# Loading the out-projection's weights into u's places during the last projection group, and 24 out-projection steps ahead of attention

## The chip, the cores and the metric

The kernel runs on one core of one Trainium2 chip. The metric is the device time of one execution in microseconds (us); lower is better. The core has five engines with a queue of their own each: TensorE (PE, with its weight loads shown as PEld), VectorE (DVE), ScalarE (ACT), GpSimd (POOL) and SyncE (SP), which here issues nearly all DMAs. An engine works through its queue in the order that was fixed when the kernel was built.

## The reference

One layer of a decoder with three parallel branches. `x` is 2048 tokens by 1024, `w_in` has 5656 columns, `w_out` is 2048 by 1024, all float32:

```
u    = rms_norm(x, norm_g)
q, k, v, z_att, f, z_ssd, xbc, dt, x_lru, z_lru = split(u @ w_in)
y_att = fox_attention(q, k, v, f) * silu(z_att)      # 8 heads of 64, causal, forget-gate bias
y_ssd = ssd(conv(xbc), dt, z_ssd), rms-normed        # 16 heads of 64, state 128
y_lru = rglru(conv(x_lru)) * silu(z_lru)             # 512 channels, a scan over time
out  = x + concat(y_att 512, y_ssd 1024, y_lru 512) @ w_out
```

## The kernel before

**Precision.** A matmul on fp32 data is made of three passes on rounded parts: a matrix is split into a high part `h` (a cast on ACT) and a low part `l` = raw - h (a subtraction on DVE or POOL), and the product is hh + hl + lh. So each weight and each input costs a cast and a subtraction before PE can use it.

**Stages.** (1) `x` is normalised, transposed and split into `uh` and `ul`: four blocks `tb` of 512 tokens, eight tiles of 128 x 512 each, 128 KB per partition in all, in the pool `up`. (2) Groups of 256 columns of `w_in` are loaded (`weights`) and multiplied with all of u, with convolutions, scans and gates behind them; results go to DRAM. (3) The SSD units. (4) For each of four pairs of heads a q/k group (tiles `pqk`, `ptq`, `sth`, `stl`) and a v/z group (`group_vz`: eight steps `t2` of 256 tokens, accumulator `pvz`, results `vs` and `zt`, stored as `v_d` and `za_d`). Steps 1 and 2 of a v/z group read u's block 0, steps 3 and 4 block 1, and so on. Three accumulator buffers (`psj`) serve these groups; `vs` has five buffers, `zt` two. (5) `pb.close()` gives back u, the weights' pools and the accumulators, and attention's pools are laid out in their place: `a4` (the logits `L`), `o2` (`mh`, `ml`, `xr`), `a2`, `a3` (`ph`, `pl`), `wo` (the split half of `w_out`, 64 KB per partition), `o1` (the raw inputs `mt`), `kvB`. (6) Attention together with the first out-projection sweep. (7) The second sweep.

**Attention.** 64 units, one for each head and block `sb` of 256 queries; heads' blocks go down (7 to 0) for the first and the last head and up for the others. `logits` makes the steps of a unit: a chunk of 512 keys at a time, PE makes `S` (L814, L815), DVE subtracts the bias and keeps the maximum (L816), ACT takes the exponential of the whole row (L820). `attend` goes over pairs of key tiles (`kp`): PE transposes `L` into `T` (L869), ACT and DVE split it into `ph` (L876) and `pl` (L877), PE multiplies with v into `O` (L855, L856), and the chunks of the next unit are put between. At the unit's end come `os`, the transposes `pf` and the sum `ats`, stored as `at_d`. The chunks of the very first unit are made with raised priority, and the keys, values and biases of the next head (`kh`, `vv`, `cb`) are loaded in each head's third unit.

**Out-projection.** `sweep` is a generator; one `next` is one step. A step multiplies one 128-row block `k` of `w_out` with a token tile's input for 256 output columns: three matmuls (L977, L979, L981) into the accumulator `po`, of which the first sweep has one (`psP`). Eight steps make one 256-wide output, which DVE adds into `xr` by two instructions (L985, L988); 32 steps make a token tile of 128. `mix` loads a tile's input (`mt`, one buffer for each half: one load from `gt_d`, four from `lr_d`), casts it to `mh` on ACT (L956) and subtracts to `ml` on POOL (L957); it is called one tile ahead. The first sweep (rows 1024 to 2047 of `w_out`: 512 steps) fills attention: after each of the 288 kp steps `fill` issues as many steps as keep it in proportion:

```
count[0] += 1
want = count[0] * 512 // 288
while want > count[1]: ... next(filler, None)
```

The generator starts, and with it `mix` of the first two tiles, at the first `fill`. The second sweep (rows 0 to 1023) has its own 512 steps after attention.

**`load_wo`** loads a half of `w_out` and splits it: eight row blocks `k`; a raw row block of 512 KB lies in the place of the next block's `wol`, the last one in the two `mt` buffers; each is split in two pieces of 512 columns (ACT L921 or L925, DVE L922 or L926). Before, it is called after the first unit's chunks and again after attention.

**Order.** All instructions are put in an order per engine by a planner that simulates the kernel with costs of its own, taking among what is ready the one that comes first in the program (raised priority counts as earlier). A tile that takes over another's place waits for that tile's last user alone (`reuse_waits`).

Of the kernel before, what the change touches and what calls it, by code (L numbers as in the profile page):

```python
# [8 lines left out]
F32 = mybir.dt.float32  # L9
F32R = mybir.dt.float32r  # L10
I32 = mybir.dt.int32
BF16 = mybir.dt.bfloat16
AF = mybir.ActivationFunctionType
ALU = mybir.AluOpType
# [4 lines left out]
P = 128  # L19
S = 2048  # L20
D = 1024
NT = S // P
# [5 lines left out]
NSL = 9  # L28
NQ = 4
QB = 5  # L30
ZPOOL = True
LORD = "x0 x1 z0 g0 x2 z1 g1 x3 z2 z3 g2 g3"
LAG = 4
# [11 lines left out]
def hybrid_block(ctx, tc, x, norm_g, w_in, q_norm_g, k_norm_g, forget_b, ssd_conv_w, ssd_conv_b,  # L45
# [3 lines left out]
    def tpool(**kw):  # L49
        if kw.get("space") is not DRAM:  # L50
            kw["reuse_waits"] = "tile"
        return tc.tile_pool(**kw)
# [100 lines left out]


    pb = ExitStack()
    up = pb.enter_context(tpool(name="up", bufs=1))
    psY = pb.enter_context(tpool(name="psY", bufs=3, space=PSUM))
    pst = pb.enter_context(tpool(name="pst", bufs=2, space=PSUM))
    psj = pb.enter_context(tpool(name="psj", bufs=3, space=PSUM))
# [2 lines left out]

    uh, ul = [], []
    for tb in range(4):
        uh.append([up.tile([P, 512], F32R, name=f"uh{tb}_{k}", tag=f"uh{tb}_{k}")
                   for k in range(KD)])
        ul.append([up.tile([P, 512], F32R, name=f"ul{tb}_{k}", tag=f"ul{tb}_{k}")
                   for k in range(KD)])
# [25 lines left out]
    with tpool(name="p0", bufs=2) as p0, tpool(name="p01", bufs=1) as p01, \  # L194
# [44 lines left out]
        def c1(name, i=0):  # L239
            j = CV[name] + i  # L240
            return cv[:, j:j + 1]
# [475 lines left out]
    def load_q(h, sb):  # L717
# [8 lines left out]
            dma(ql[u * 64:u * 64 + 64, :].bitcast(F32), qk_d["q", "l", p][hs, qs])  # L726
        heads[h][3:] = [qh, ql]

    with tpool(name="ap", bufs=2) as pool, tpool(name="ap1", bufs=1) as ap1, \
            tpool(name="qkp", bufs=QB) as qkp:  # L730
        for p in range(4):
            w = weights([(C_Q + p * P, P), (C_K + p * P, P)])
            for th in range(8 // NQ):
                ss = pool.tile([P, NQ, 8], F32, name=f"sqk{p}_{th}", tag="sqk")
                rs = pool.tile([P, NQ, 8], F32, name=f"rqk{p}_{th}", tag="rqk")
                qks = []
                for i in range(NQ):
                    t2 = th * NQ + i
                    qk = qkp.tile([P, 2, 256], F32, name=f"qk{p}_{t2}", tag="qk")
                    qks.append(qk)  # L740
                    ps = proj_tok2(w, t2, f"pqk{p}_{t2}")
                    A.copy(qk, ps)
                    sq = ap1.tile([P, 2, 256], F32, name=f"sq{p}_{t2}", tag="sqq")
                    A.activation(sq, ps, AF.Square)
                    V.tensor_reduce(ss[:, i, :], sq.rearrange("p i (h d) -> p (i h) d", d=64),
                                    axis=AX.X, op=ALU.add)
                s2_, r2_ = (z.rearrange("p a b -> p (a b)") for z in (ss, rs))
                V.tensor_scalar(s2_, s2_, 1.0 / 64.0, EPS, op0=ALU.mult, op1=ALU.add)
                rsqrt(ap1, r2_, s2_, NQ * 8, f"rk{p}{th}")
                for i, qk in enumerate(qks):  # L750
                    t2 = th * NQ + i
                    qv = qk.rearrange("p i (h d) -> p (i h) d", d=64)
                    V.tensor_tensor(qv, qv, rs[:, i, :].unsqueeze(2).broadcast_to([P, 8, 64]),
                                    op=ALU.mult)
                    pt = pst.tile([P, 2, 256], F32, name=f"ptq{p}_{t2}", tag="pt")
                    for j in range(2):
                        for i2 in range(2):
                            T.transpose(pt[:, j, i2 * P:(i2 + 1) * P],
                                        qk[:, i2, j * P:(j + 1) * P], ident)
                    ts = slice(t2 * 256, (t2 + 1) * 256)  # L760
                    for j, (wn, gn) in enumerate((("q", "qg"), ("k", "kg"))):
                        sh = pool.tile([P, 256], F32R, name=f"sth{p}_{t2}_{j}", tag="sth")
                        sl = pool.tile([P, 256], F32R, name=f"stl{p}_{t2}_{j}", tag="stl")
                        A.activation(sh, pt[:, j, :], AF.Copy, scale=c1(gn))
                        V.scalar_tensor_tensor(sl, pt[:, j, :], c1(gn), sh.bitcast(F32),
                                               op0=ALU.mult, op1=ALU.subtract)
                        dma(qk_d[wn, "h", p][:, ts], sh.bitcast(F32))
                        dma(qk_d[wn, "l", p][:, ts], sl.bitcast(F32))
            if p > 0:
                group_vz(pool, qkp, p)  # L770
            if p == 2:
                load_head(0)
                load_q(*units[0])
    pb.close()

    pcx = ExitStack()
# [1 line left out]
    o2 = cx.enter_context(tpool(name="o2", bufs=2))  # L778
    a2 = cx.enter_context(tpool(name="a2", bufs=2))
    a3 = cx.enter_context(tpool(name="a3", bufs=3))  # L780
    wo = cx.enter_context(tpool(name="wo", bufs=1))
    o1 = cx.enter_context(tpool(name="o1", bufs=1))
    kvB = cx.enter_context(tpool(name="kvB", bufs=1))
    psS = pcx.enter_context(tpool(name="psS", bufs=PB[0], space=PSUM))
# [115 lines left out]

    pt_d = dram("pt_d", [S, D])

    def load_wo(ks):
        w = {}
        for j, k in enumerate(ks):
            h = wo.tile([P, D], F32R, name=f"woh{k}", tag=f"woh{j}")
            l = wo.tile([P, D], F32R, name=f"wol{k}", tag=f"wol{j}")
            row = w_out[k * P:(k + 1) * P, :]
            if j < 7:
                whole = wo.tile([P, D], F32, name=f"wor{k}", tag=f"wol{j + 1}")  # L910
                dma(whole, row)
            for n in range(2):
                cs = slice(n * 512, n * 512 + 512)
                if j < 7:
                    raw = whole[:, cs]
                else:
                    raw = o1.tile([P, 512], F32, name=f"wor{k}_{n}", tag=f"mt{n}")
                    dma(raw, row[:, cs])
                if 4 <= k < 12:
                    g = c1("sg", k - 4)  # L920
                    A.activation(h[:, cs], raw, AF.Copy, scale=g)  # L921
                    V.scalar_tensor_tensor(l[:, cs], raw, g, h[:, cs].bitcast(F32),  # L922
                                           op0=ALU.mult, op1=ALU.subtract)
                else:
                    A.copy(h[:, cs], raw)  # L925
                    V.tensor_tensor(l[:, cs], raw, h[:, cs].bitcast(F32),  # L926
                                    op=ALU.subtract)
            w[k] = (h, l)
        return w

    def sweep(w, psP, psX, parts, resid, dst, ts):


# [27 lines left out]
        for i, t in enumerate(ts):  # L961
            nxt = mix(ts[i + 1]) if i + 1 < NT else None
            tsl = slice(t * P, (t + 1) * P)
            mh, ml = cur
            for n in range(4):
                cs = slice(n * 256, n * 256 + 256)
                if n % 2 == 0:
                    xr = o2.tile([P, 512], F32, name=f"xr{t}_{n}_{ks[0]}", tag="xr")
                    dma(xr, resid[tsl, n * 256:n * 256 + 512])
                xc = xr[:, n % 2 * 256:n % 2 * 256 + 256]  # L970

                ps = psP.tile([P, 2, 256], F32, name=f"po{t}_{n}_{ks[0]}", tag="P")
                for j, k in enumerate(ks):
                    yield
                    h, l = w[k]
                    o = ps[:, j // 4, :]
                    T.matmul(o, mh[:, j, :], h[:, cs], start=(j == 0), stop=False,  # L977
                             skip_group_check=True)
                    T.matmul(o, mh[:, j, :], l[:, cs], start=False, stop=False,  # L979
                             skip_group_check=True)  # L980
                    T.matmul(o, ml[:, j, :], h[:, cs], start=False, stop=(j % 4 == 3),  # L981
                             skip_group_check=True)
                for j, (kind, _) in enumerate(parts):
                    if kind in (0, 1):
                        V.scalar_tensor_tensor(xc, ps[:, j, :], rsn[:, t, kind:kind + 1], xc,  # L985
                                               op0=ALU.mult, op1=ALU.add)
                    else:
                        V.tensor_tensor(xc, xc, ps[:, j, :], op=ALU.add)  # L988
                if n % 2:
                    dma(dst[tsl, n * 256 - 256:n * 256 + 256], xr)  # L990
            cur = nxt

    with tc.high_priority(offset=HP):
        cur, steps = logits(*units[0])
        for st in steps:
            st()
    w = load_wo(range(8, 16))
    filler = sweep(w, psP, None, ((1, 8), ("lru", 12)), xf, pt_d, range(NT))
    count = [0, 0]
    recent = []  # L1000

    def fill(ins):
# [14 lines left out]
    pcx.close()  # L1017
    psP2 = cx.enter_context(tpool(name="psP2", bufs=5, space=PSUM))
    psX = cx.enter_context(tpool(name="psX", bufs=3, space=PSUM))
    w = load_wo(list(range(4, 8)) + list(range(0, 4)))  # L1020
    for _ in sweep(w, psP2, psX, ((0, 4), ("att", 0)), pt_d, of, range(NT - 1, -1, -1)):
        pass
    cx.close()

# [28 lines left out]
```

## Time and profile before

| | us |
|---|---|
| median of 3 runs (2082.02, 2083.0, 2092.18) | 2083.0 |
| the profiled execution | 2094.4 |
| its span, first to last instruction | 2092.4 |
| PE busy in it | 2011.2 |
| DVE busy | 1278.1 |
| ACT busy | 954.3 |
| POOL busy | 542.0 |
| first start and last end of a split instruction of w_out, first half | 1276.7 and 1297.6 |
| last v/z result taken by ACT | 1275.49 |
| first out-projection matmul | 1306.7 |
| first out-projection matmul of the second sweep | 1898.12 |

All numbers come from one profiled execution, which is 0.5% above the median of the runs. Times inside are counted from the first instruction. Busy time of an engine counts its instructions alone; a busy PE isn't PE at its peak, since matmuls overlap and run at half speed where the granted clock is 0.50. Rows of DMAs on SP (SPq) show the issue, not the transfer.

### The profile page before, as it was taken

Reading aid. Unit: us, or ns where it says so; the run is one execution under the profiler, and the core shown is the slowest. Engines: PE = TensorE matmul, PEld = TensorE weight load, DVE = VectorE, ACT = ScalarE, POOL = GpSimd, SP = SyncE. Lnnn points to the kernel's source line nnn. Section 1 sums busy time; section 2 is a strip of 40 time slices with the busy share of each in tenths; the row PEclk is TensorE's granted clock in tenths of the full one; section 3 lists DMA queues with packets and bytes.
Section 4 is the critical chain, followed back from the end, with each engine's and each line's share of the span. In section 5 each row is a group of like instructions: output and inputs, shape, how many; then the busy total and the mean of one; then the engine's idle time right before and its main releaser. Section 6 shows DMA issues by size and latency. Waiting matters only on the chain. (4 is left out here: it accounts for less than half of the span.)

```text
span 2092.4 us, 38943 instructions
## 1 busy us (share of the span) xinstructions
PE 2011.2 (96%) x14021; PEld 1838.4 (88%) x14021; DVE 1278.1 (61%) x2844; ACT 954.3 (46%) x1985; POOL 542.0 (26%) x750
## 2 busy tenths in 40 slices
PE   7999999999999999998999998999999999998999
PEld 6788888887789998887888996989999999997999
DVE  6654555488874226767576245677787787774333
ACT  8444443466642215454444234566556565652100
POOL 0000001355531004454552001342233323121110
PEclk9999999999999999999999999999999999998999
DMA  5122233111123225666655636365435535234443
GB/s 195 41 71 61 71 112 93 42 42 42 42 72 98 82 80 165 188 182 197 190 166 177 167 116 205 100 165 144 116 110 147 132 105 155 64 100 139 137 133 106
DMA packets 277826, 248.59 MB, mean 119 GB/s; under 512 B 58725, under 2 KB 225153, under 8 KB 275585
## 3 DMA queue, kind: packets, MB, share of 16 engines
q1 hardware_dynamic: 277472, 246.07, 40.6%
q8 instruction: 111, 1.82, 0.4%
q0 software_dynamic: 160, 0.03, 0.1%
q14 instruction: 83, 0.67, 0.1%
HBM read 159.83 MB, written 86.18 MB: 118 GB/s over the span
## 5 line engine op out<-in xcount | busy, mean ns | idle before, releaser
L977 PE MATMUL po<-woh,mh 128*128 128x256 f32 x1024 | 295.2, 289 | 7.3 <-ACT mh L956 7.3
L981 PE MATMUL po<-woh,ml 128*128 128x256 f32 x1024 | 289.3, 283 | 0.0
L979 PE MATMUL po<-wol,mh 128*128 128x256 f32 x1024 | 288.2, 282 | 0.0
L876 ACT CAST ph<-T 128x512 fp32r<-128x512 f32 (+2 forms) x352 | 163.4, 490 | 144.4 <-PE T L869 79.7
L877 DVE TENSOR_TENSOR pl<-T,ph 128x512 fp32r<-128x512 f32 (+2 forms) x352 | 191.0, 563 | 32.5 <-ACT ph L876 32.2
L977 PEld LDWEIGHTS po<-woh,mh 128*128 128x128 f32 x1024 | 193.8, 189 | 10.4 <-ACT mh L956 8.0
L979 PEld LDWEIGHTS po<-wol,mh 128*128 128x128 f32 x1024 | 194.4, 190 | 2.7
L981 PEld LDWEIGHTS po<-woh,ml 128*128 128x128 f32 x1024 | 193.4, 189 | 1.0
L820 ACT ACTIVATE L<-L,mx 128x1920 f32<-128x1920 f32 (+15 forms) x128 | 154.7, 1209 | 54.6 <-DVE mx L819 39.0
L869 PE MATMUL T<-ident,L 128*128 128x128 f32 x1088 | 175.6, 276 | 1.2 <-ACT L L820 0.8
L373 DVE SCALAR_TENSOR_TENSOR accx<-rtx,cv,accx 128x512 f32<-128x512 f32 x144 | 104.6, 752 | 90.4 <-ACT accx L370 76.2
L855 PE MATMUL O<-ph,vv 128*128 128x256 f32 x576 | 154.7, 288 | 3.0 <-ACT ph L876 3.0
L322 PE MATMUL pxx<-uh,wh 128*128 128x512 f32 x384 | 152.7, 400 | 4.7 <-ACT rtx L365 3.3
L856 PE MATMUL O<-pl,vv 128*128 128x256 f32 x576 | 154.1, 291 | 1.0 <-DVE pl L877 0.9
L323 PE MATMUL pxx<-ul,wh 128*128 128x512 f32 x384 | 153.4, 400 | 0.0
L313 PE MATMUL pqk<-wl,uh 128*128 128x256 f32 x512 | 152.6, 299 | 0.8 <-DVE wl L187 0.8
L324 PE MATMUL pxx<-uh,wl 128*128 128x512 f32 x384 | 152.3, 398 | 0.0
L312 PE MATMUL pqk<-wh,uh 128*128 128x256 f32 x512 | 147.8, 293 | 3.0 <-ACT wh L186 3.0
L809 POOL TENSOR_SCALAR_AFFINE_SELECT cm<-cb 128x384 f32<-128x384 f32 (+3 forms) x128 | 58.7, 460 | 352.8 <-DVE mx L816 229.9
L314 PE MATMUL pqk<-wh,ul 128*128 128x256 f32 x512 | 149.5, 294 | 0.0
L313 PE MATMUL pzs<-wl,uh 128*128 128x256 f32 x512 | 144.5, 284 | 3.2 <-POOL wl L187 3.2
L314 PE MATMUL pzs<-wh,ul 128*128 128x256 f32 x512 | 144.4, 283 | 0.0
(313 smaller groups left out, 5661.2 us busy)
## 6 DMA issues: line engine op xcount, KB each, us to landing
ab<-acs_d SPq DMA_DIRECT2D x64, 256.0 KB
wr<-in_w_in_dram SPq DMA_DIRECT2D x192, 64.0 KB
wr<-in_w_in_dram SPq DMA_DIRECT2D x80, 128.0 KB
xt<-in_x_dram SPq DMA_DIRECT2D x16, 512.0 KB
xs_d<-stx SPq DMA_DIRECT2D x32, 256.0 KB
v_d<-vs SPq DMA_DIRECT2D x32, 256.0 KB
zs_d<-zs SPq DMA_DIRECT2D x32, 256.0 KB
xs<-xs_d SPq DMA_DIRECT2D x32, 256.0 KB
```

The lines of the kernel that those rows point to most:

```text
L313: T.matmul(ps[:, i, :], h[k][:, sl], wl[k], start=False, stop=False)
L314: T.matmul(ps[:, i, :], l[k][:, sl], wh[k], start=False, stop=(k == KD - 1))
L323: T.matmul(ps, wh[k][:, ms], ul[tb][k], start=False, stop=False)
L820: A.activation(lt[:, 0:n], lt[:, 0:n], AF.Exp, bias=mx, accum_out=sm[:, i:i + 1])
L855: T.matmul(po[:, ca], vv[:, kt, :], ph[:, jj, ca], start=(kt == 0), stop=False)
L856: T.matmul(po[:, ca], vv[:, kt, :], pl[:, jj, ca], start=False, stop=(kt == nk - 1))
L869: ins = T.transpose(pt[:, jj, i * P:(i + 1) * P], L[i][:, kt * P:(kt + 1) * P], ident)
L876: A.copy(ph[:, ja, ca], pt[:, ja, ca])
L877: V.tensor_tensor(pl[:, ja, ca], pt[:, ja, ca], ph[:, ja, ca].bitcast(F32), op=ALU.subtract)
L977: T.matmul(o, mh[:, j, :], h[:, cs], start=(j == 0), stop=False, skip_group_check=True)
L979: T.matmul(o, mh[:, j, :], l[:, cs], start=False, stop=False, skip_group_check=True)
L981: T.matmul(o, ml[:, j, :], h[:, cs], start=False, stop=(j % 4 == 3), skip_group_check=True)
```

## The change

The pool of u is cut in two: `upa` holds blocks 0 and 1 and stays open to the kernel's end, `upb` holds blocks 2 and 3 and is given back as before. `load_wo` is called for the first sweep's half right after the last v/z group, before `pb.close()`, and takes tiles of 128 x 512 in `upa` by the very tags of u's tiles, so that each piece waits for one or two tiles of u alone. A raw piece (256 KB) lies in the place of the next piece's `wol`; the last one comes as two halves in another pool (the weights' raw buffer the first time, the one `mt0` buffer the second time). The pool `wo` is gone, and attention's pools begin where u's third block was. The matmuls read the same numbers from the new tiles. And 24 steps are taken from the sweep ahead of the first unit's `attend`, `count` starting at 24.

```diff
+FIRST = 24
...
-    up = pb.enter_context(tpool(name="up", bufs=1))
+    upa = ctx.enter_context(tpool(name="upa", bufs=1))
+    upb = pb.enter_context(tpool(name="upb", bufs=1))
...
+        up = upa if tb < 2 else upb
...
+    def load_wo(ks, lastp, tag):
+        ws = {}
+        pl = [(k, n) for k in ks for n in range(2)]
+        tags = [f"u{p}{tb}_{k}" for tb in range(2) for k in range(KD) for p in "hl"]
+        for j, (k, n) in enumerate(pl):
+            h = upa.tile([P, 512], F32R, name=f"woh{k}_{n}", tag=tags[2 * j])
+            l = upa.tile([P, 512], F32R, name=f"wol{k}_{n}", tag=tags[2 * j + 1])
+            cs = slice(n * 512, n * 512 + 512)
+            row = w_out[k * P:(k + 1) * P, cs]
+            if j + 1 < len(pl):
+                raw = [upa.tile([P, 512], F32, name=f"wor{k}_{n}", tag=tags[2 * j + 3])]
+            else:
+                raw = [lastp.tile([P, 256], F32, name=f"wor{k}_{n}_{i}", tag=tag) for i in range(2)]
+            m = 512 // len(raw)
+            for i, r in enumerate(raw):
+                dma(r, row[:, i * m:(i + 1) * m])
+                hc, lc = h[:, i * m:(i + 1) * m], l[:, i * m:(i + 1) * m]
+                if 4 <= k < 12:
+                    g = c1("sg", k - 4)
+                    A.activation(hc, r, AF.Copy, scale=g)
+                    V.scalar_tensor_tensor(lc, r, g, hc.bitcast(F32), op0=ALU.mult,
+                                           op1=ALU.subtract)
+                else:
+                    A.copy(hc, r)
+                    V.tensor_tensor(lc, r, hc.bitcast(F32), op=ALU.subtract)
+            ws[k, n] = (h, l)
+        return ws
...
+    w1 = load_wo(range(8, 16), wrp, "wr")
     pb.close()
...
-    wo = cx.enter_context(tpool(name="wo", bufs=1))
...
-                    h, l = w[k]
+                    h, l = w[k, n // 2]
+                    wc = slice(n % 2 * 256, n % 2 * 256 + 256)
...
-    w = load_wo(range(8, 16))
-    filler = sweep(w, psP, None, ((1, 8), ("lru", 12)), xf, pt_d, range(NT))
-    count = [0, 0]
+    filler = sweep(w1, psP, None, ((1, 8), ("lru", 12)), xf, pt_d, range(NT))
+    for _ in range(FIRST):
+        next(filler)
+    count = [0, FIRST]
...
-    w = load_wo(list(range(4, 8)) + list(range(0, 4)))
-    for _ in sweep(w, psP2, psX, ((0, 4), ("att", 0)), pt_d, of, range(NT - 1, -1, -1)):
+    w2 = load_wo(list(range(4, 8)) + list(range(0, 4)), o1, "mt0")
+    for _ in sweep(w2, psP2, psX, ((0, 4), ("att", 0)), pt_d, of, range(NT - 1, -1, -1)):
         pass
```

More of the change, by code (lines that the diff above doesn't have):

```diff
@@ L901, in hybrid_block @@
     pt_d = dram("pt_d", [S, D])
[L903 to L929, printed above, removed]
     def sweep(w, psP, psX, parts, resid, dst, ts):
@@ L965, in sweep @@
             for n in range(4):
-                cs = slice(n * 256, n * 256 + 256)
                 if n % 2 == 0:
@@ L974, in sweep @@
                     yield
-                    h, l = w[k]
+                    h, l = w[k, n // 2]
+                    wc = slice(n % 2 * 256, n % 2 * 256 + 256)
                     o = ps[:, j // 4, :]
-                    T.matmul(o, mh[:, j, :], h[:, cs], start=(j == 0), stop=False,
+                    T.matmul(o, mh[:, j, :], h[:, wc], start=(j == 0), stop=False,
                              skip_group_check=True)
-                    T.matmul(o, mh[:, j, :], l[:, cs], start=False, stop=False,
+                    T.matmul(o, mh[:, j, :], l[:, wc], start=False, stop=False,
                              skip_group_check=True)
-                    T.matmul(o, ml[:, j, :], h[:, cs], start=False, stop=(j % 4 == 3),
+                    T.matmul(o, ml[:, j, :], h[:, wc], start=False, stop=(j % 4 == 3),
                              skip_group_check=True)
```

## The prediction

> **What bounds the kernel now.** I read the page first, then the busy times by stretch of time, then the chain of work where TensorE has holes. On the page:
>
> ```profile
> span 2092.4 us, 38943 instructions
> PE 2011.2 (96%) x14021; PEld 1838.4 (88%) x14021; DVE 1278.1 (61%) x2844; ACT 954.3 (46%) x1985; POOL 542.0 (26%) x750
> ```
>
> TensorE (PE) is busy 96% of the span, so the change can only win where PE has holes. Next the stretches around the end of the last v/z group, near 1275.2 us. The columns are: stretch, length, busy us and count of PE, PEld (weight loads), DVE, ACT, POOL, then granted PE clock, DMA share, GB/s.
>
> ```profile
> 1250.00:1260.00 10.00, 10.00 (x87) 10.00 (x86) 2.34 (x6) 1.54 (x4) 1.08 (x2) 1.00 0.30 100
> ...
> 1276.00:1280.00 4.00, 2.44 (x8) 1.19 (x8) 3.79 (x12) 2.65 (x4) 0.30 (x1) 1.00 0.83 260
> 1280.00:1285.00 5.00, 2.90 (x11) 1.28 (x9) 4.83 (x11) 4.62 (x8) 0.85 (x1) 0.99 1.00 389
> 1285.00:1290.00 5.00, 3.84 (x14) 3.12 (x15) 5.00 (x14) 4.91 (x9) 0.49 (x1) 0.50 1.06 392
> 1290.00:1295.00 5.00, 3.93 (x16) 2.19 (x14) 5.00 (x12) 5.00 (x10) 2.76 (x3) 0.83 1.05 278
> 1295.00:1300.00 5.00, 4.11 (x29) 3.51 (x30) 5.00 (x13) 1.38 (x3) 0.04 (x1) 1.00 1.07 225
> 1300.00:1305.00 5.00, 4.06 (x31) 3.52 (x29) 4.32 (x14) 2.63 (x4) 1.43 (x3) 1.00 0.67 167
> 1305.00:1310.00 5.00, 2.04 (x9) 1.52 (x10) 1.17 (x2) 2.92 (x6) 2.82 (x3) 0.88 0.60 153
> 1310.00:1315.00 5.00, 5.00 (x23) 4.70 (x23) 1.81 (x7) 3.00 (x5) 1.65 (x2) 0.50 0.28 81
> ```
>
> The reader is to see four things: before 1275 PE is full and DVE, ACT and DMA are nearly idle; from 1280 to 1300 DVE and DMA are full instead, ACT too until 1295; from 1305 to 1310 nobody works much; and in two stretches the clock is at half (0.50). What stood in the way is in the chain of waits:
>
> ```profile
> 1296.34 1.28 DVE wol L926 x2
> ...
> 1300.41 5.55 DMA mt<-gt_d
> ...
> 1306.65 0.38 PE po L977
> ```
>
> The last split of w_out (`wol`) ends late, only then is the buffer `mt` free for the first out-projection input, whose load takes 5.55 us among the other traffic, and the first out-projection step (`po`) starts at 1306.65.
>
> How much does that stretch lose? I take one milestone: first two attention units done and the first 24 steps (three of the 256-wide outputs of the first token tile) added into `xr`. Before, that is at 1328.9, the start of the third L988 add, quoted further down. The first row is everything from 1275.20 to there (PE, PEld, DVE, ACT, POOL as above), the next four PE's work on po, S, T and O, in this order, with its count:
>
> ```profile
> 1275.20:1328.90 53.70, 42.93 (x254) 35.05 (x253) 39.67 (x99) 32.43 (x55) 12.94 (x17) 0.87 0.68 203
> 1275.20:1328.90 53.70, 11.28 (x72) 10.39 (x72) 2.28 (x5) 0.87 0.68 203
> 1275.20:1328.90 53.70, 17.27 (x46) 7.99 (x46) 16.09 (x24) 0.87 0.68 203
> 1275.20:1328.90 53.70, 12.14 (x71) 9.61 (x72) 11.25 (x19) 9.55 (x19) 0.87 0.68 203
> 1275.20:1328.90 53.70, 10.75 (x60) 8.56 (x60) 0.44 (x2) 0.87 0.68 203
> ```
>
> What these cost on a busy PE at full clock, from the chain in the middle of attention:
>
> ```profile
> 1790.38 0.23 PE S L814
> ...
> 1790.85 0.12 PE po L977
> ...
> 1791.66 0.11 PE O L855
> ...
> 1792.23 0.44 PE T L869 x4
> ```
>
> So the work is 46 x 0.23 + 72 x 0.12 + 60 x 0.115 + 71 x 0.11 = 10.6 + 8.6 + 6.9 + 7.8 = 33.9, with the few `pf` transposes 34.0 us. The stretch takes 53.7 us, so 19.7 us are lost. That is all the change can win here.
>
> **The change part by part.**
>
> *The split of the first half of w_out moves from after the last v/z group into it.* Its instructions, counted over both halves of w_out, so that one half has 8 of each row:
>
> ```profile
> L921 ACT ACTIVATE woh<-wor,cv x16: 704/718/733, 1276.7 to 1886.3; 128x512 fp32r<-128x512 f32 x16
> L922 DVE SCALAR_TENSOR_TENSOR wol<-wor,cv,woh x16: 737/744/943, 1279.5 to 1887.6; 128x512 fp32r<-128x512 f32 x16
> L925 ACT CAST woh<-wor x16: 600/619/635, 1287.4 to 1889.8; 128x512 fp32r<-128x512 f32 x16
> L926 DVE TENSOR_TENSOR wol<-wor,woh x16: 665/679/939, 1289.3 to 1893.6; 128x512 fp32r<-128x512 f32 x16
> L911 SPq DMA_DIRECT2D wor<-in_w_out_dram x14: 346/418/682, 1272.5 to 1878.4; - x14
> ```
>
> ACT: 8 x 0.72 + 8 x 0.62 = 10.7 us; DVE: 8 x 0.74 + 8 x 0.68 = 11.4 us; 4.2 MB of loads. u's first two blocks have their last readers in steps 2 and 4 of the last group's eight. The results of steps 4 and 8 are taken here:
>
> ```profile
> 1252.77 0.38 ACT L345 ACTIVATE vs<-pvz 128x256 fp32r<-128x256 f32 x1 [4.20 <-PE pvz L314]
> ...
> 1275.49 0.38 ACT L345 ACTIVATE vs<-pvz 128x256 fp32r<-128x256 f32 x1 [4.42 <-PE pvz L314]
> ```
>
> So a step takes 5.7 us, all the new places are free by 1252.8, and 22 us remain, in which DVE works 2.34 and ACT 1.54 of 10 us and DMA 0.30. The moved work fits and costs nothing there; its cover is PE's matmuls of the group. SP gets 17 issues instead of 9, about 0.42 us each (8 more: 3.4 us). Queued behind a load that waits for its place are the `v_d` and `za_d` stores; `vs` has five buffers and `zt` two, and PE has two spare accumulators, so a wait is harmless up to about two steps of 5.7 us. I take nothing, bounds 0 to 2 us.
>
> *What goes with it:* DVE has 28.3 us to do until the milestone instead of 39.7, against 34.0 for PE, so DVE stops being the bound. The `mt` buffers no longer hold raw w_out, so the first input can be loaded when v/z's weights are released, about 1275.
>
> *24 steps ahead of the first unit.* 72 matmuls, 8.6 us of PE, move from between kp steps (attention's steps of two key tiles) to the hole after 1275. With them come two inputs `mix` (10 loads on SP, 4 casts on ACT, 4 subtractions on POOL), two `xr` loads, one store, and six adds on DVE:
>
> ```profile
> L956 ACT CAST mh<-mt x4: 617/620/625, 1306.0 to 1317.0; 128x512 fp32r<-128x512 f32 x4
> L957 POOL TENSOR_TENSOR ml<-mt,mh x4: 1268/1294/1307, 1306.7 to 1317.7; 128x512 fp32r<-128x512 f32 x4
> ...
> L985 DVE SCALAR_TENSOR_TENSOR xr<-po,rsn,xr x3: 484/485/485, 1316.7 to 1328.0; 128x256 f32<-128x256 f32 x3
> L988 DVE TENSOR_TENSOR xr<-xr,po x3: 403/417/422, 1317.7 to 1328.9; 128x256 f32<-128x256 f32 x3
> ...
> 1894.45 2.98 DMA mt<-gt_d
> ```
>
> The last row is the same load with little other traffic: 2.98 us. What PE still loses until the milestone, term by term:
>
> (a) Until the first step can run: 1275.5 + 2.98 + 0.62 + 1.29 = 1280.4, 5.2 us after the last v/z matmul; PE has about ten matmuls of the first unit's S in it, 2.2 us. Loss 3.0 (2 to 4).
>
> (b) The steps share one `po` accumulator; each of three outputs waits for 0.49 + 0.41 on DVE. Two can be covered by S and T, so 0.9 (0 to 2.7).
>
> (c) The first 14 fill calls now add no step (24 is ahead of 14 x 512/288). Without steps PE needs per kp step 0.44 + 4 x 0.115 + 2 x 0.23 = 1.36 us. DVE's share is seen here, by start times:
>
> ```profile
> 1297.54 0.74 DVE L816 CUSTOM_DVE_ANT_0 L<-S,cb,mx 128x512 f32<-128x512 f32 x1
> ...
> 1298.21 1.28 DVE L877 TENSOR_TENSOR pl<-T,ph 128x512 fp32r<-128x512 f32 x2
> ```
>
> 0.67 for a chunk of S and about 0.61 for `pl`, 1.28 with some small ones: as much as PE. Lower end nothing. Upper end: the pace that it has with steps, 1.36 + 1.78 x 0.36 = 2.0 us, so 14 x 0.64 = 9.0. DVE's row is nearest to the lower end; for hand-overs I take 2.5.
>
> (d) The second input loads beside head 1's 3 MB, and ACT stands before its cast. Between 0 and the 5.55 us of that row; I take 1.5, as ACT's work can go ahead in its planned order.
>
> (e) Half clock: before, two stretches of about 7 us. PE's holes are now shorter than 6 us, where before PE was thinly used from 1276 to 1285 before the clock fell; I take 0.5 (0 to 3.5, half of one such stretch). The Trainium skill, TensorE: Matmul & The Clock Gate, Part 1, says that one idle window of about 3.4 us halves the clock. By that rule term (a)'s hole would cost half of such a window, an estimate of 1.7 us instead of 0.5, and the time would be 1.2 us later; the trace kept 1.00 for 1276 to 1280 with weight loads busy 1.19 of 4 us, and fell only at 1285.
>
> Sum 3.0 + 0.9 + 2.5 + 1.5 + 0.5 = 8.4 us lost instead of 19.7: a gain of 11.3 us.
>
> *The second half of w_out, between the sweeps.*
>
> ```profile
> 1878.00:1902.70 24.70, 12.85 (x63) 10.90 (x62) 15.82 (x32) 14.02 (x32) 7.28 (x9) 0.65 0.59 198
> ...
> 1878.61 0.72 ACT L921 ACTIVATE woh<-wor,cv 128x512 fp32r<-128x512 f32 x1 [1.00 <-DMA wor<-in_w_out_dram]
> ```
>
> With half-row tiles, eight of sixteen raw pieces have free places 16 steps earlier, so ACT needn't wait for a landing and may begin some 3 us sooner. Against it, the last piece goes as two halves through one `mt0` buffer, so one more landing (2.98) stands before the second sweep's first input. Bounds -3 to +3; neither row is nearer, I take 0.
>
> **Sum.** The profiled execution takes 2094.4 us and would take 2083.1. The median shown is 2083.0, the profiled one being 11.4 above it; the same gain gives 2071.7.
>
> **The rivals.**
>
> *R1, the stretch without steps runs at the old pace* (term c at its upper end, 9.0): for it speaks that ACT and DVE wait for each other in each kp step; against it DVE's 1.28 us. Gain 4.8 us, 2078.2.
>
> *R2, the steps don't run early.* If SP issues head 1's 3 MB (`cb`, `kh`, `vv`, 128 x 2048 fp32 each) before the first `mt` load, that is 8.0 us at 390 GB/s from about 1278.5, and `mt` lands 5.55 later at 1292, its steps start at 1294. If PE's order has them ahead of the first T, PE loses 16.4 instead of 3.0, gain -2.1: 2085. Against it: `mt`'s place comes free with the weights, before the `v_d` stores that head 1's tiles wait for. Each us after 1294 is a us more; slower by over 0.5% from 1302 on.
>
> *R3, slower: the order of the whole attention is planned anew, and head loads hit it.* Before, one of the later head loads stalls PE:
>
> ```profile
> 1370.00:1380.00 10.00, 7.45 (x51) 5.76 (x50) 7.19 (x30) 5.85 (x17) 5.01 (x12) 1.00 0.80 202
> ```
>
> 2.55 us. If the new order does that at the other five, 12.8 us are lost: 2084.5. It decides from five such stalls on; with stalls as long as the 5.55 us load it would be 2099. Against it: from the 15th fill call on the steps come as before.
>
> *R4, smaller loads.* The w_out loads go from 512 to 256 KB. If the late 2 MB between the sweeps go at half of the 390 GB/s, they take 10.8 instead of 5.4 us; some 1.4 us of that lie beside ACT's work on the pieces that are there already, and the second sweep starts 4 us later: 2075.7. For it: the lone 256 KB `mt` load above moved at 88 GB/s. Against it: loads queue up one behind the other here. The Trainium skill, SBUF — State Buffer, "The DMA setup-cost knee", gives 224 GB/s at 256 KiB and 341 at 1 MiB for a transfer by itself; by that the same loads take an estimated 9.4 us.
>
> **How the numbers follow.** Forecast 0.52, R1 0.22, R2 0.10, R3 0.10, R4 0.06. The bound of 0.5% is 10.4 us, about what a measurement here tells from no change: under 2072.6 is faster, over 2093.4 slower. The forecast's own range is 2062 (all terms at their lower ends, gain 17.7, and 3 us between the sweeps) to 2074; 0.06 of its 0.52 lies above 2072.6, so faster 0.46. Slower is half of R3 and 0.03 of R2: 0.08. Same 0.46. The range reaches over R1 and R4 to R2 and R3's centres: 2062 to 2086.
>
> **What would show it.** Right: the first half's `woh` and `wol` end before 1275; the first `po` at about 1280; no `wol` between 1280 and 1300, DVE below 0.9 there; clock 1.00 in nearly all stretches; the milestone near 1317. Wrong: `po` after 1290 (R2), holes of PE from the milestone's start at every kp step (R1), waits at `cb`, `kh`, `vv` loads (R3), or a late `mt` load between the sweeps (R4); or PE holes before 1275, which the forecast holds to be nothing.

## The result and the profile after

The change made the kernel slightly slower, not faster: 2091.22 us (median of 22 runs, 2085.34 to 2098.42) against 2084.39 us (22 runs, 2077.14 to 2092.18) before, a ratio of 1.0034 with a 95% interval of 1.0023 to 1.0045. Run again on another occasion beside other runs of before, the same kernel took 2091.23 us against 2086.73, ratio 1.0022 (1.0004 to 1.0040). So it lost 4.5 to 7 us where the forecast had it gain 11.3. Both ratios are under the 0.5% that the prediction called about what a measurement here tells from no change; with this many runs the intervals still show a small loss.

The top of the page of the profiled execution, which took 2085.63 us, 5.6 us less than the median:

```profile
span 2083.8 us, 38989 instructions
PE 2009.7 (96%) x14021; PEld 1840.9 (88%) x14021; DVE 1281.1 (61%) x2846; ACT 953.1 (46%) x1987; POOL 539.6 (26%) x750
```

Nothing here tells where time was lost, so the busy times by stretch are next (columns as in the prediction). The last v/z matmul is at 1268.7.

```profile
1250.00:1260.00 10.00, 10.00 (x87) 10.00 (x87) 5.91 (x10) 6.68 (x13) 0.00 (x0) 1.00 0.98 335
...
1268.70:1275.00 6.30, 4.63 (x24) 2.88 (x24) 4.81 (x14) 3.78 (x6) 1.61 (x3) 1.00 0.69 204
1275.00:1280.00 5.00, 4.33 (x29) 3.66 (x27) 3.68 (x13) 1.84 (x3) 2.73 (x3) 1.00 0.90 274
...
1290.00:1295.00 5.00, 3.04 (x26) 2.80 (x25) 0.00 (x0) 0.15 (x1) 0.00 (x0) 1.00 0.99 264
1295.00:1300.00 5.00, 3.65 (x17) 3.26 (x18) 2.79 (x8) 2.08 (x5) 1.89 (x2) 0.75 0.39 118
```

The splits of w_out do fit beside the last v/z group: ACT, DVE and DMA work there and PE keeps its 87 matmuls in 10 us. PE has work again at once. What is new is the stretch from 1290 to 1295: DVE and ACT stand still while DMA is full. ACT's rows in order of time say for what:

```profile
1287.70 0.59 ACT L909 CAST ph<-T 128x512 fp32r<-128x512 f32 x1 [0.56 <-PE T L902]
1294.85 0.62 ACT L961 CAST mh<-mt 128x512 fp32r<-128x512 f32 x1 [6.57 <-DMA mt<-lr_d]
```

ACT stood 6.57 us at the cast of the second token tile's input, whose four loads queue behind head 1's 3 MB, and attention's `ph` stood behind it. In the other profiles of the change's order with one buffer for each `mt` tile the same wait is 3.0 to 6.7 us.

Between the sweeps, the chain of waits and ACT's rows:

```profile
1879.95 0.36 SPq L929
...
1880.40 2.88 DMA mt<-at_d
...
1884.90 3.02 DMA mt<-gt_d
...
1888.61 0.58 PE po L982
```

```profile
1883.63 0.41 ACT L757 CAST woh<-wor 128x256 fp32r<-128x256 f32 x1 [3.66 <-DMA wor<-in_w_out_dram]
1887.94 0.62 ACT L961 CAST mh<-mt 128x512 fp32r<-128x512 f32 x1 [3.91 <-DMA mt<-gt_d]
```

Two landings follow one another in the one `mt0` buffer: the second half of the last raw piece, and only when that is split the second sweep's first input from `gt_d`. The chain shows another landing in the place of the first, that of the input from `at_d` in the other buffer, `mt1`: it ran beside the raw piece's, and SP has the next tile's load into `mt1` ahead of the load from `gt_d`. Its transposes ended at 1884.46 and the split of the raw piece at 1884.49, so the two hold up the load from `gt_d` alike.

The third loss can't be seen in a busy column. These are the rows of `po` alone on PE in the same 100 us of the second sweep: before, before in a second profile, and after.

```profile
1950.00:2050.00 100.00, 98.46 (x821) 1.00 0.45 137
```

```profile
1950.00:2050.00 100.00, 98.27 (x850) 1.00 0.46 138
```

```profile
1950.00:2050.00 100.00, 98.46 (x807) 1.00 0.44 135
```

The busy share is 98% in all three, at full clock, and nobody waits; but 821 or 850 matmuls were done before and 807 after. By their start times, from one to the next it is 117.78 ns in the first profile of before, 113.55 in the second (once settled 113.3), and 119.98 after.

The stages of all kernels below, from those profiles' start times, in us. *A*: from the last v/z matmul to the end copy `os` of attention's ninth unit; *B*: on to that of the last unit; *C*: on to the second sweep's first `po`; *D*: on to the end. *po* is the mean of the steady distances of `po` matmuls in the second sweep, in ns (at the slowest pace the first few of a tile come closer together, and the mean over all is 119.9). Each ratio is to runs of before on the same occasion, whose medians lie between 2084.39 and 2089.80 us, so times of different rows compare by their ratios.

| kernel | median us (runs) | ratio to before (95%) | A | B | C | D | po |
|---|---|---|---|---|---|---|---|
| before | 2084.39 (22) | | 103.9 | 513.2 | 5.8 | 194.3 | 117.78 |
| b0, before again | 2087.46 (8) | 1.0007 (0.9988–1.0026) | 101.5 | 515.4 | 5.8 | 187.4 | 113.55 |
| after | 2091.22 (22) | 1.0034 (1.0023–1.0045) | 93.3 | 515.3 | 11.3 | 195.2 | 119.98 |
| a0, after again | 2091.23 (12) | 1.0022 (1.0004–1.0040) | 88.7 | 515.4 | 11.4 | 196.0 | 119.98 |
| first0 | 2091.60 (12) | 1.0013 (0.9996–1.0030) | 90.3 | 515.9 | 9.9 | 196.9 | 119.9 |
| mt2 | 2090.89 (12) | 1.0013 (0.9996–1.0030) | 94.2 | 515.4 | 6.5 | 198.0 | 119.9 |
| bfirst | 2087.15 (12) | 1.0001 (0.9980–1.0021) | 98.8 | 512.8 | 5.9 | 194.4 | 117.78 |
| bpad | 2094.66 (6) | 1.0051 (1.0036–1.0066) | 99.6 | 515.4 | 5.8 | 197.1 | 119.98 |
| amtb | 2086.66 (11) | 1.0006 (0.9997–1.0016) | 88.8 | 515.5 | 6.8 | 197.2 | 119.98 |
| ap64 | 2086.93 (12) | 0.9989 (0.9972–1.0007) | 92.1 | 512.5 | 11.2 | 193.0 | 117.78 |
| aw64 | 2081.15 (12) | 0.9967 (0.9950–0.9984) | 91.6 | 512.1 | 11.2 | 187.1 | 113.61 |
| mp64 | 2076.40 (7) | 0.9953 (0.9934–0.9972) | 89.0 | 512.8 | 6.7 | 192.8 | 117.78 |
| eq32 | 2093.64 (10) | 1.0020 (1.0003–1.0036) | 93.5 | 515.2 | 11.3 | 196.5 | 120.00 |
| mw64 | 2073.16 (5) | 0.9925 (0.9899–0.9952) | 87.5 | 512.5 | 6.8 | 187.8 | 113.61 |
| mw128 | 2083.16 (10) | 0.9978 (0.9962–0.9994) | 88.5 | 515.4 | 6.9 | 194.2 | 118.66 |
| mw256 | 2083.87 (10) | 0.9975 (0.9962–0.9988) | 88.6 | 515.4 | 6.6 | 196.0 | 119.97 |
| bm64 | 2082.90 (12) | 0.9974 (0.9959–0.9988) | 101.0 | 512.2 | 5.9 | 187.2 | 113.33 |

The change wins some 9 us in A (92.2 on the mean of after, `a0`, `mt2`, `ap64`, `aw64` and `eq32`, against 101.0 of the five profiles in before's order) and gives them back in B, C and D. (b0's B holds a stretch of 6.8 us at half clock that the other kernels of that order don't have.) The last v/z matmul itself lies between 1268.7 and 1280.8 in these profiles with no order between the kernels: what is ahead of it varies by some 6 us either way from run to run, so single profiles are compared by stages.

### The profile page after: what moved, and what is told of

It reads as the page before. It is cut to its first block, busy times and chain, and to the rows that moved or that the text cites. A ratio compares the mean times of both kernels' runs of the same rounds, so it can differ in the third digit from the quotient of the medians.

```text
span 2083.8 us, 38989 instructions
## 1 busy us (share of the span) xinstructions
PE 2009.7 (96%) x14021; PEld 1840.9 (88%) x14021; DVE 1281.1 (61%) x2846; ACT 953.1 (46%) x1987; POOL 539.6 (26%) x750
## 5 line engine op out<-in xcount | busy, mean ns | idle before, releaser
L982 PEld LDWEIGHTS po<-woh,mh 128*128 128x128 f32 x1024 | 196.0, 191 | 4.1 <-ACT mh L961 1.3
```

The costliest lines, as they stand in the source:

```text
L982: T.matmul(o, mh[:, j, :], h[:, wc], start=(j == 0), stop=False, skip_group_check=True)
```

## The experiments

**Two suspects in the code.** `mt2`: the last raw piece's halves get two buffers; `first0`: the 24 early steps are left out; `bfirst`: the kernel before with the 24 steps alone; `a0`: the changed kernel again, unedited.

```diff
# mt2                                   # first0          # bfirst (on the kernel before)
-    ... o1, "mt0")                     -FIRST = 24       +    for _ in range(24):
+    ... o1, ("mt0", "mt1"))            +FIRST = 0        +        next(filler)
                                                          -    count = [0, 0]
                                                          +    count = [0, 24]
```

> The changed kernel, but the two halves of the last raw piece go to two buffers, mt0 and mt1, as before the change. Theory A: the second sweep's first input is loaded right after the last attention store, so W to X falls by 4 to 5 us to about 20, and so does the time. Theory B: W to X may fall, but the time stays within 2 us of the changed kernel, since what is lost is lost earlier.

> The changed kernel with FIRST = 0: w_out's first half in u's places, but the steps start at the first fill call as before. Theory A: the split's move alone gains in V to W (DVE and ACT free after 1275: 5 us or more against 602.6), W to X stays at 25. Theory B: without the early steps V to W is shorter than with them, by up to 5 us, and so is the time. If the early steps are what gains, V to W is 3 to 9 us longer than in the changed kernel.

> The kernel before with the 24 early steps alone, w_out loaded in its old place (its loads and splits end at 1297, so the steps can't run before). Theory B (early steps hurt): slower than before by 5 us or more, PE's queue standing at the steps until mt is loaded, V to W over 607. Theory A: W to X 20 as before, time within 3 us of before or slower only through V to W.

> The changed kernel as it is, for a second profile of it. In the first profile three stretches were measured: from the last v/z matmul (V) to the first sweep's last step (W) 594.6 us against 602.6 before, from there to the second sweep's first step (X) 25.3 against 20.3, and from X to the end 195.2 against 194.3; together 2.1 us gained, where the medians lose 7. Theory A (the loss lies between the sweeps, the last raw piece of w_out going twice through one mt0 buffer): W to X again 25 us or longer. Theory B (the 24 early steps and the 14 calls without steps don't gain in a typical execution): V to W about 600 or longer, W to X as before. Both: time 5 to 9 us over the kernel before.

`a0` was 4.5 us over the before of its occasion, just short of the 5 to 9 expected, and V to W (W is the first sweep's last `po`) was 589.9 us, so theory B is out; W to X was 25.6, as theory A had it. `mt2` took C from 11.3 to 6.5 us, so the one buffer is what C lost; its median is only 0.3 us under that of `a0`, as its theory B had it. Part of what C wins comes back in D: the second sweep's first tile took 12.8 and 13.5 us in after and `a0`, whose transposes `px` were made while PE waited in C, and 15.5 in `mt2`. `first0` is no different from `a0`: with w_out's splits in their new place, the 24 early steps decide nothing that can be told. `bfirst` can't speak on the steps: the planner left all 14,021 matmuls and transposes in the order of before, and its first `po` is at 1310.6, 29.8 us after the last v/z matmul (31.5 in before). None of the three explains the loss, and the difference of 2 to 6 ns in `po` stood in every one of these profiles with the new places of w_out.

**The place alone.** Per partition, w_out's first tile begins at byte 95,776 before and 20,960 after, the first `mh` at 53,728 and 119,264. Modulo 512, `mh` and `ml` stay at 480, and so do the other tiles of attention; w_out's tiles alone go from 32 to 480. `bpad` gives the kernel before that remainder; `apad` gives the changed kernel the old one; `amtb` takes up the wait in A with two buffers for `mt`; `best` joins the last two.

```diff
# bpad (before)                     # apad (after; both pads on u's level)     # amtb (after)
+    pad of 448 bytes               +    pad of 64 bytes                       -    o1: bufs=1
     wo = ...                            upa = ...                             +    o1: bufs=2
+    pad of 64 bytes                +    pad of 448 bytes
```

> The kernel before with one edit: 448 bytes of padding per partition ahead of w_out's tiles and 64 behind them, so that the tiles begin 480 bytes past a multiple of 512, as they do after the change, instead of 32 past one; order of work and all other places modulo 512 stay. In every trace so far the steady distance from one po matmul to the next is 117.7 ns in the kernels with the tiles at 32 (mean of 1528 in before) and 119.95 ns in those with them at 480 (1532 in after). Theory 'place': po goes to 119.9 ns here too, 3072 x about 2 ns = 5 to 6 us longer than before, about 1.0027. Rival 'half rows' (tiles of 512 instead of 1024 columns make the difference): po stays at 117.7 and the time at before's.

> The kernel after with 64 bytes of padding ahead of u's first two blocks and 448 behind them: w_out's half-row tiles begin 32 past a multiple of 512, as before the change. Theory 'place': po at 117.7 ns instead of 119.95, 5 to 6 us faster than after, about 2085, level with before. Rival 'half rows': po stays at 120 and the time at 2091. The projections that read u's first two blocks may change their distance too (118.2 ns now), by at most the same 2 ns either way: bounds of plus or minus 4 us before the last v/z matmul.

> The kernel after with two buffers instead of one for each mt tile (nothing else): the second input can be loaded before head 1's cb, kh and vv, and the last raw piece of the second half of w_out has two places. Theory 'mt': the wait of the second input's cast (6.57 us on DMA in after) goes, V to W becomes 3 to 6 us shorter, W to X goes from 25 to 20 or 21 us; together 5 to 10 us faster than after, 2081 to 2086. Rival 'covered': as with mt2, what is won at these places comes back as later waits, and the time stays at 2090 within 2 us.

> Padding of apad and the two mt buffers of amtb together. If both theories hold: 5 to 6 us for the place and 5 to 10 for the buffers, 2075 to 2081, under before by 4 to 10 us. If only 'place' holds: 2085. If neither: 2090.

`bpad` does everything as before, in the order of before but for eight matmuls at one place of a q/k group, and is 0.51% slower (9.6 us at the medians), more than the whole change costs; `po` in it stands as after:

```profile
1950.00:2050.00 100.00, 98.46 (x808) 1.00 0.44 136
```

So the half rows are not it, the place is. 3072 x 2.2 ns is 6.8 us against the first pace of before; against the second the second sweep alone loses 1536 x 6.4 ns, some 10 us.

`apad` missed: 2183.54 us, ratio 1.047, and `best` 2174.04. Their `po` did fall (113.85 and 117.78 ns), but the two pads together gave the planner another order of the state-space stage. The stretch 900 to 950, first `apad`, then after:

```profile
900.00:950.00 50.00, 37.16 (x155) 24.08 (x156) 29.37 (x42) 21.52 (x63) 32.80 (x36) 0.80 0.60 179
```

```profile
900.00:950.00 50.00, 46.15 (x336) 40.33 (x335) 37.39 (x71) 26.16 (x74) 23.07 (x25) 1.00 0.62 181
```

PE got half as many matmuls there, which put the last v/z matmul 100 us later; it says nothing on the question. `amtb` held its theory: the wait of 6.57 us is 1.05, seen here, and C is 6.8.

```profile
1285.67 0.62 ACT L961 CAST mh<-mt 128x512 fp32r<-128x512 f32 x1 [1.05 <-DMA mt<-lr_d]
```

It is 4.6 us under after at the medians, just short of the 5 to 10 expected, and by the ratios (1.0006 against 1.0022 and 1.0034) 3 to 6 us.

**The place, with the order kept.** `ap64` moves w_out's tiles to 32 with the second pad put behind attention's `a4`, which leaves the state-space stage's order alone (u's tiles and `a4` move by the same 64 bytes); `aw64` moves `mh` and `ml` to 32 instead; `mp64` is `ap64` with `amtb`'s buffers; `b0` is the kernel before.

```diff
# ap64, mp64 (after, amtb)           # aw64 (after)
+    pad of 64 bytes                 +    pad of 64 bytes
     upa = ...                            o2 = ...
...                                  +    pad of 448 bytes
+    pad of 448 bytes
     o2 = ...
```

> The kernel after with 64 bytes of padding ahead of u's first two blocks, and 448 more ahead of the tiles of the out-projection's inputs (mh, ml): w_out's tiles begin 32 past a multiple of 512 as before the change, mh and ml 480 past one as always. Unlike the run with both pads ahead of and behind u's blocks, the order of the state-space stage stays that of after. Theory 'place': po falls from 119.98 to 117.8 ns (or to the 113.9 ns that the second sweep had in that run), V to end is 6 to 13 us shorter than after's 811 to 815 us, and the time 6 to 10 us under after: 2081 to 2085, at or just under before. Rival 'half rows': po at 120, 2091.

> The kernel after with 64 bytes of padding ahead of mh and ml alone: w_out's tiles (what streams) stay at 480 past a multiple of 512, the weights that are loaded (mh, ml) go from 480 to 32. If the place of what streams sets the distance, po stays at 119.98 ns and the time at 2091; if the two must not begin at the same place modulo 512, po falls to 117.8 or less and the time to 2081 to 2085.

> ap64 with two buffers for each mt tile. If both theories hold: 6 to 10 us under the 2086.7 us of the kernel with two mt buffers alone, 2077 to 2081, 4 to 8 us under before, near the forecast's 11 us gain only if po goes below 117.8 ns. Rival: the shorter po steps come back as waits for DVE and ACT in attention, where PE is not alone at its limit, and only the 3 us of the second sweep are won: 2084.

> The kernel before once more, for a second profile of it: the first was taken in an execution 10 us above the median. If the stage that the change touches was what made it long, V to W (602.6 us there) is 592 to 597 here; if the early stages made it long, V to W stays at 602 and V comes earlier than 1275. W to X 20.3 and X to end 194.3 us should stay within 0.5 us.

B is back at 512.1 to 512.8 us and `po` at 117.78 or 113.61 ns in all three, whichever operand was moved. `ap64`'s median, 2086.93 us, is still 2 us above the range expected, and `aw64`'s is at the range's lower end. `mp64` at 2076.4 us is 0.47% faster than before. `b0` missed in an instructive way: D was to stay within 0.5 us of 194.3 and was 187.4, the same kernel at another pace; V to W was 602.4 us once more. The start times show how: a token tile of the second sweep runs at 117.8 or 113.3 ns throughout, and the pace changes only at a tile's beginning, where PE makes the four transposes `px` of a coming input and two `po` start 0.47 us apart, the next 0.20 us on. `before` stayed at 117.8 through all 16 tiles, `b0` went to 113.3 after its first.

**The rule.** `eq32` puts w_out's tiles and `mh`, `ml` all at 32; `mw64`, `mw128` and `mw256` put `mh` and `ml` 64, 128 and 256 bytes further than in `amtb`; `bm64` gives the kernel before w_out's tiles 64 bytes below `mh` and `ml` (modulo 512) instead of 64 above.

```diff
# eq32 (after)            # mw64, 128, 256 (amtb)           # bm64 (before)
+    pad of 64 bytes      +    pad of 64, 128, 256 bytes    +    pad of 384 bytes
     upa = ...                 o2 = ...                          wo = ...
     o2 = ...             +    pad of 448, 384, 256 bytes   +    pad of 128 bytes
+    pad of 448 bytes
```

> The kernel after with 64 bytes of padding ahead of u's first two blocks and 448 behind mh and ml: w_out's tiles and mh, ml all begin 32 past a multiple of 512. If it is the common remainder that costs, po is back at 119.98 ns and the second sweep at 195 to 198 us, time about 2091. If 480 as the place of what streams costs, po is at 117.8 or 113.6 ns and the time 2080 to 2087.

> Two mt buffers, and 64 bytes of padding ahead of mh and ml (w_out's tiles at 480, mh and ml at 32). Expected like the kernel with the same distance made at w_out's tiles: po 117.8 or 113.6 ns, 2076 us within 3, V to W 588, W to X 21.

> Two mt buffers, and 128 bytes of padding ahead of mh and ml (w_out's tiles at 480, mh and ml at 96). If any distance will do, po is at 117.8 or 113.6 ns and the time 2076 within 3; if the pace falls with the distance, po is at or under 113.6 in the whole second sweep, X to end 187 us, 2070 to 2074.

> Two mt buffers, and 256 bytes of padding ahead of mh and ml (w_out's tiles at 480, mh and ml at 224, the farthest apart modulo 512). If any distance will do, as with 128 bytes: 2076 within 3. If the rule goes by 256, this is as bad as a common place: po 119.98 ns and 2086.7 as with two mt buffers alone. If farther is better, po at 113.6 or less and 2070 to 2074.

> The kernel before with padding of 384 bytes ahead of w_out's tiles and 128 behind: what streams begins 64 bytes below mh and ml modulo 512 instead of 64 above, nothing else changed. If the sign decides which of the two paces is taken, the second sweep is at 113.6 ns, X to end 187 us and the time 3 to 5 us under before (half of before's runs have that pace already), which leaves 10 to 12 us of mw64's lead to the change and its buffers. If the sign does not matter: before's time within 2 us, and the whole of the lead is the change's.

The rows of `po` in the same 100 us, `eq32`, `mw64`, `mw128`, `mw256`, `bm64`:

```profile
1950.00:2050.00 100.00, 98.46 (x807) 1.00 0.44 137
```

```profile
1950.00:2050.00 100.00, 98.27 (x848) 1.00 0.42 132
```

```profile
1950.00:2050.00 100.00, 98.46 (x816) 1.00 0.42 128
```

```profile
1950.00:2050.00 100.00, 98.31 (x804) 1.00 0.43 130
```

```profile
1950.00:2050.00 100.00, 98.27 (x848) 1.00 0.47 142
```

A common remainder costs wherever it is (`eq32`), and so does a distance of 256 (`mw256`, expected only by one of its three readings); 128 is between, 64 is best. With w_out 64 below, the second sweep of `bm64` ran at 113.3 ns in every tile, and those of `aw64` and `mw64` in all but one of their 16; with 64 above, five of seven profiles never left 117.8 (before, `bfirst`, `ap64`, `best`, `mp64`), and `b0` and `apad` changed early. The medians agree: the ratio falls from 1 to 0.9974 (before, `bm64`), from 0.9989 to 0.9967 (`ap64`, `aw64`) and from 0.9953 to 0.9925 (`mp64`, `mw64`). So the sign sways the pace, and before gains 0.26% by `bm64`'s padding alone. `mw128`, at 2083.16 us, met neither of its two readings.

That gives the change its price at an equal place: `aw64` against `bm64` is 0.9967 to 0.9974, and `ap64` against before 0.9989 (0.9972 to 1.0007), no difference that can be told. In the stages `aw64` wins 9.4 us in A and loses 5.3 in C. With two `mt` buffers, `mw64` to `bm64` is 0.9925 to 0.9974, 0.5% or some 10 us. `mw64` beats both kernels: 2073.16 us, 0.75% under the 2089.37 us of before on the same occasion.

## Why the prediction was wrong

**The steps that held.** The split fits beside the last v/z group and costs nothing there that can be told from the spread ahead of it. The steps run early: the first `po` came 3.8 us after the last v/z matmul (forecast 5.2 for the first step), so R2 is out. From the last v/z matmul to the milestone (two units done and 24 steps added) it took 47.6, 42.7, 47.1, 45.2, 46.0 and 47.8 us in the profiles of after, `a0`, `mt2`, `aw64`, `ap64` and `eq32`, 46.1 on the mean, where the forecast had 53.7 - 11.3 = 42.4. The baseline was long: 53.7 in the first profile of before, but 51.4 in `b0`, 51.2 in `bm64`, 49.8 in `bpad` and 49.0 in `bfirst`, 51.0 on the mean of the five. So the gain at the milestone was 4.9 us, less than half of the forecast's. Up to the ninth unit it is 8.7 us (92.2 against 101.0): where the gain comes from was right, and its size three quarters of what the forecast took. No new stall came at the later heads (B is the same for equal places), so R3 is out; R4's slow loads weren't seen either (295 GB/s from 1865 to 1870 in after, where R4 had 195). R1 is out as well: with two `mt` buffers, where the wait of term (d) is at most 1.05 us, the stretch to the milestone takes 41.6 us on the mean and so loses 41.6 - 34.0 = 7.6, where R1 with nothing for (d) would lose 13.4.

**The step that failed first** was no term but the price under all of them: the prediction took 0.12 us a `po` from a row of before and let all 3072 `po` matmuls keep it, though the change gives w_out's tiles other places. They went to 119.98 ns. That costs 3.0 us in B (515.3 against the 512.3 of `ap64` and `aw64`), as `bpad` with its 515.4 shows by itself, and in D 2.8 or 9.7 us by `bpad` (197.1 against 194.3 or 187.4). In the D of after, `a0` and `eq32` (195.9 on the mean) 1.6 or 8.5 us of it show, the transposes `px` of the first tile having been made in C. No rival had it.

**The second** was "neither row is nearer, I take 0" for the second half of w_out, with bounds of 3 us either way. C went from 5.8 to 11.3 us, 5.5 us and outside the bounds. The prediction did name the mechanism, one more landing in the one `mt0` buffer; what it left out is that this landing's own issue stands behind the last unit's `ats` and its store on SP, at 1879.95, so that two landings and a split come after attention's end instead of one. Two buffers gave 4.5 us of C back (`amtb`). Taken to the end of the second sweep's first tile, so that the transposes count alike, it is 24.1 and 25.0 us in after and `a0` against 20.5 in `bpad`, 3.6 to 4.5 us lost and still outside the bounds; `amtb` has 21.2.

**The third** is term (d), 1.5 us taken for the second input. The runs with two `mt` buffers reach the milestone at 41.3, 42.2, 42.1, 41.5 and 41.0 us (`amtb`, `mp64`, `mw64`, `mw128`, `mw256`) instead of 46.1: 4.5 us, inside its bounds, but with a wait on ACT that is above the 5.55 taken for the upper end in four of the six profiles above (6.57 in after). "ACT's work can go ahead in its planned order" was the wrong reason: the planned order had the cast ahead of attention's `ph`.

Term (e) and the rule beside it: in after the clock stayed at 1.00 through the hole of the first 6.3 us, where PEld worked 2.88 us, and fell in 1295 to 1300, after the wait of ACT. By the rule of the Trainium skill (TensorE: Matmul & The Clock Gate, Part 1) as the prediction read it, that hole would have cost half a window at half clock. The trace of after doesn't show it, and neither do six others in the change's order, but five do: in `first0`, `mt2`, `mp64`, `eq32` and `mw64` the clock was at 0.50 for 3.4 us, beginning 3.7 to 4.5 us after the last v/z matmul. PE's longest idle time there was 1.1 us in all twelve, so this price differs from execution to execution; as an estimate, five in twelve times half of 3.4 us is 0.7 us, near the 0.5 taken.

Adding the stages, -8.7 in A, +2 to 3 in B, +5.5 in C and on the mean of before's two paces +5.0 in D give +3.8 to +4.8 us, and the medians +4.5 to +6.8. What is left is less than A alone varies by from profile to profile (88.7 to 94.2 us with one buffer), and what share of before's runs has the faster pace single profiles can't give; this stays open.

## What to carry to other kernels

Moving a tensor is a change of its own: before a forecast keeps a duration for a matmul whose operand moves, compare where the streamed operand and the weights begin, and after the run count matmuls in a stretch of equal length, because the busy share can't show a pace. When a buffer is shared by the end of one job and the start of the next, count every landing through it together with what stands ahead of its issue on the queue. An input loaded ahead needs a place of its own ahead of the large loads, or the engine that waits for it holds up the work behind it.

## What the hardware showed that was not expected

With 256-wide fp32r matmuls, each with its own weight load, the steady distance depends on how far apart modulo 256 bytes the streamed operand and the weights begin in a partition: 119.98 ns at 0 (after, `bpad`, `eq32`, `mw256`), 118.66 at 128, 117.78 or 113.3 at 64. Other distances weren't tried, and that 256 counts like 0 rests on `mw256` alone. At a distance of 64 there are two paces, 4% apart, and one can change into the other where the four transposes at a tile's start come between; why it does in some tiles and not in others is open. From `bpad` to `bm64`, which differ in nothing but w_out's place, it is 1.0051 to 0.9974 of before, some 16 us of this kernel's 2085, and the two paces are part of why its runs differ: before's D is 194.3 or 187.4 us.

The Trainium skill, SBUF — State Buffer, "Who interferes with whom", gives TensorE two independent read ports, one for the moving operand and one for the weight load, and says that it never waits for anyone. In these runs the pace followed the two places alone while the other engines' work and order stayed as they were, which fits that as far as other engines go; but the two streams of TensorE itself are not independent of each other's place. That they meet inside the memory would explain it and isn't shown.
